# Eight conditioning dots moved from the pair stage into the middle output projection of a two-layer decoder trunk

## The chip, the cores and the metric

The kernel runs on one core of one Trainium2 chip. The metric is device microseconds of one execution. Engines are named as the profile names them: PE (TensorE matmul), PEld (its weight loads), DVE (VectorE), ACT (ScalarE), POOL (GpSimd), SP (SyncE, which only issues transfers here).

## What is computed

The reference runs two layers over x (512 tokens, 1024 channels). What matters here is the second layer:

```python
m = silu(c) @ ada_w[1] + ada_b[1]          # c: one vector of 1024
shift, scale, gate = split(m, 3)           # 1024 each
h = rmsnorm(x) * (1 + scale) + shift
gb, gc, u, g = split(h @ odd_w_in, 4)      # 2048 channels each
y = gb * (conv_b + conv3(gc * u)) * silu(g)
x = x + (1 + gate) * (y @ odd_w_out)
```

`gate` is read first where the output projection is added to x.

## The kernel before

Everything lies transposed: channels on the 128 partitions, 512 tokens along the free axis. The 2048 inner channels of layer 1 are 16 blocks j of 128. For each block four products of 128x1024 weights with h are needed. All matmuls are done in three passes on two-part numbers (hi·hi, hi·lo, lo·hi), so every weight tile is first split: ACT casts the high part, DVE subtracts to get the low part (`hilo`, L60 and L61).

**The stages of layer 1.** Blocks 0 and 1 are computed tile by tile (`classic`). From block 2 on, two weight tiles at a time form a pair and go through seven smaller products of 12 matmuls each in place of eight (`load_pair`, `prep`, `product`, `step`). A block has two pairs, the even one (gate gc and u, which ends in the convolution, `done_a`) and the odd one (gb and g, which ends in `done_b`: SiLU on ACT, two multiplications and a split on DVE). So a block is 2 x 7 x 12 = 168 matmuls of 256 columns. The order of the products is the list `order`. After the odd pair of block 8 (called the seam here; it is pair 13 of 0 to 26) the first half of the output projection stands in the list: eight tiles `("out", 0)` to `("out", 7)`, each of 24 matmuls of 512 columns, each followed by `x_add` (L225), which adds the result, scaled by the gate column of that tile, to x. Then pairs 14 to 26 follow, and the second half of the projection.

**A pair's transfers.** SP issues r2 (L879, 512 KB), r1 (L880, 512 KB) and r3 (L881, 256 KB); POOL issues one more of 512 KB that adds into r2 (L882, called the accumulating transfer here). r1 shares three buffers with the tiles of the output projection (`raw`, L74 and L75), r2 has two buffers and r3 has two. The split of a product's weights is prepared up to six steps ahead of its matmuls, into six buffers.

**The dots.** One dot of the conditioning is one row block of 128 of `silu(c) @ ada_w`: a transfer of 512 KB into one of three `araw` buffers (L107, SP), a multiply-and-sum over 128x1024 on DVE (L114) with a small read of its sum, and for the gate an addition of 1 (L124). 40 of the 48 dots are done before layer 1's pair stage. The last eight, the gate's, are done one after each of blocks 0 to 7: `ada_next(1)` in `classic` (L1015) and in `done_b` (L1031) issues the load and the dot together.

**What sets the order.** PE and SP run in the order in which the program is written. ACT, DVE and POOL are ordered by the framework's planner from its own estimates of when things are ready, and then each engine works its list in that order. `ada_dot(..., True)` pins the dot behind the DVE instruction written just before it; after a block that is the split of the block's result (`yl`, L61).

Of the kernel before, what the change touches and what calls it, by code (L numbers as in the profile page):

```python
# [37 lines left out]
class Trunk:  # L38
# [939 lines left out]
    def layer1(self):  # L978
        nc = self.nc
        ha, hb = slice(0, 256), slice(256, S)  # L980
        ra = self.ra
        hf = [self.ap.tile([P, 2, S], F32, tag="sf"[i % 2], name="hf", bufs=2) for i in range(4)]
        self.hf = [hf[k // 2][:, k % 2] for k in range(KT)]

        ws = [self.next_unit(0) for _ in range(4)]
        pj = [self.mbank() for _ in range(2)] + [self.zbank() for _ in range(2)]
        for half, sl in enumerate((ha, hb)):
            for k in range(KT):
                t = self.h_scale(1, k, ra, sl)
                self.h_hi(1, k, t, sl)  # L990
                self.h_lo(1, k, t, sl)
                nc.scalar.activation(self.hf[k][:, sl], t, AF.Identity, bias=self.adacol(1, 0, k))
                c = slice(k * P, (k + 1) * P)
                for (wh, wl), ps in zip(ws, pj):
                    self.mm3(ps[:, sl], wh[:, c], wl[:, c], self.hh[k][:, sl], self.hl[k][:, sl], k == 0, k == KT - 1)
                if half == 0 and k == 2:
                    rb = self.second()
                if half == 1 and k < 4 and k % 2:
                    self.split_upto(self.used + k // 2 + 1, True)
            ra = rb  # L1000
        ys = {}

        def classic(j, get, acc=None, sums=None):
            if acc is None:
                pc = get()
                gc = self.t512("t")
                nc.scalar.copy(out=gc, in_=pc)
                acc = self.conv(j, gc, get())
            if sums:
                sums()  # L1010
            pg = get()
            sg = self.t512("sga")
            nc.scalar.activation(sg, pg, AF.Silu)
            ys[j] = self.gated(acc, get(), sg)
            self.ada_next(1)  # L1015
            return sg

        classic(0, lambda: pj.pop(0))
        accs = {}
        self.prod_no = 0  # L1020

        def done_a(j):
            def f(gc, u):
                accs[j] = self.conv(j, gc, u)
            return f

        def done_b(j):
            def f(gb, gate):
                nc.scalar.activation(gate, gate, AF.Silu)
                ys[j] = self.gated(accs.pop(j), gb, gate)  # L1030
                self.ada_next(1)  # L1031
            return f

        pairs = []
        for j in self.PAIRED:
            pairs.append(dict(m=(16 + j, 32 + j), tag="t", done=done_a(j), odd=0, j=j))
            if j < 15:
                pairs.append(dict(m=(j, 48 + j), tag="sga", done=done_b(j), odd=1, j=j))

        order = []  # L1040
        for i, pr in enumerate(pairs):
            last = pairs[i - 1] if i else None
            order += [(pr, 1), (pr, 5)]
            if last and not last.get("early"):
                order += [(last, 4)]
            order += [(pr, 6), (pr, 2)]
            if last and not last.get("early"):
                order += [(last, 3)]
            order += [(pr, 7)]
            if pr["j"] == 8 and pr["odd"]:  # L1050
                pr["early"] = True
                order += [("out", 0), (pr, 4), (pr, 3)] + [("out", mt) for mt in range(1, 8)]
        order += [("tail", 0), (pairs[-1], 4), (pairs[-1], 3)]
        loaded = [0]

        def load_to(n):
            while loaded[0] < min(n, len(pairs)):
                pr = pairs[loaded[0]]
                pr.update(self.load_pair(*pr["m"]))
                loaded[0] += 1  # L1060

        classic(1, self.mtile, sums=lambda: (self.make_t(), load_to(1)))
        load_to(2)
        prepped = 0

        hold = [1 + next(i for i, pr in enumerate(pairs) if pr["j"] == 8 and pr["odd"])]
        for i, (pr, n) in enumerate(order):

            while prepped < min(len(order), i + 6):
                q, m = order[prepped]  # L1070
                if not isinstance(q, str):
                    if m == 1:
                        load_to(min(pairs.index(q) + 2, hold[0]))
                    if "r1" not in q:
                        break
                    self.prep(q, self.WEIGHT[m])
                prepped += 1
            if pr == "out":
                if n == 0:
                    self.limit += 8  # L1080
                if n == 6:
                    hold[0] = len(pairs)
                    load_to(loaded[0] + 1)
                w = self.next_unit(1)
                ps = self.mbank()
                self.out_mm(ps, w, [ys[q] for q in range(8)], range(8))
                self.x_add(1, n, ps)
            elif pr == "tail":
                self.limit = len(self.units)
            else:  # L1090
                self.step(pr, n)
        sg = classic(15, self.mtile, accs.pop(15))
        ys = [ys[q] for q in range(8, 16)]
        self.preload_rsqrt(sg[:, 0:1])
        ra, second = self.outproj_norm(1, ys, keep=True)

        fg = lambda k: self.cst[:, C_FG + k : C_FG + k + 1]

        def scale(k, sl):
            x = self.x[k][:, sl]  # L1100
            nc.scalar.activation(x, x, AF.Copy, scale=fg(k))

        for half, sl in enumerate((ha, hb)):
            gps = (2, 3, 4, 5) if half == 0 else (3, 4)
            tags = (("khe", "kho", "kle", "klo"), ("qe", "qo", "s", "f"))[half]
            o = [self.ap.tile([P, 2, 256], F32, tag=t, name="o", bufs=2 if t in "sf" else 1) for t in tags]
            for k in gps:
                scale(k, sl)
            if half:
                ra = second()  # L1110
            for k in (0, 3, 1, 2, 4, 5, 6, 7):
                d, x = o[k // 2][:, k % 2], self.x[k][:, sl]
                if k in gps:
                    nc.gpsimd.tensor_tensor(out=d, in0=x, in1=ra[0], op=ALU.mult)
                else:
                    nc.vector.scalar_tensor_tensor(d, x, fg(k), ra[1], ALU.mult, ALU.mult)
            for q in range(4):
                (nc.scalar if half and q == 2 else nc.sync).dma_start(self.io["out"][half, q], o[q])
# [60 lines left out]
```

## Time and profile before

| what | us |
|---|---|
| median of 3 runs (887.85 to 890.38) | 889.59 |
| the profiled execution's own time | 890.67 |
| its span, first to last instruction | 888.9 |
| mean granted TensorE clock, share of full | 0.992 |

Times in the trace count from the start of the span. In it `classic` for blocks 0 and 1 fills about 440 to 488, the pairs before the seam 488 to 649, the middle output projection 644 to 690, the pairs behind it 690 to 812. An engine's busy time counts what its instructions cover; matmuls overlap, so 100% of PE is no sign that it runs at its best rate. A wait is the idle time of an engine before an instruction, with the name of what ended it.

### The profile page before, as it was taken

How to read it: one execution, taken by the hardware profiler on the slowest of the kernel's cores; microseconds unless marked ns; L12 is line 12 of the kernel's file. 1: busy time of each engine (PE TensorE's matmuls, PEld its weight loads, DVE VectorE, ACT ScalarE, POOL GpSimd, SP SyncE). 2: the span in 40 equal slices, each digit the busy share in tenths (PEclk: the TensorE clock that was granted, in tenths of full speed). 3: DMA queues.
4: the chain of work that ended last, by engine and by line, in shares of the span. 5: the costliest groups of instructions: out<-in, count | busy, mean ns of one | idle time of the engine just before them, and what ended most of it. 6: DMA issues, size and time to landing. Idle time of an engine off the chain costs nothing.

```text
span 888.9 us, 13496 instructions
## 1 busy us (share of the span) xinstructions
PE 860.7 (97%) x5149; PEld 765.5 (86%) x5150; DVE 685.5 (77%) x1091; ACT 450.7 (51%) x821; POOL 88.0 (10%) x133
## 2 busy tenths in 40 slices
PE   8999999999999999999999899889999999999995
PEld 5788788888888888888998899889988999999885
DVE  7989978788877787695669788778854688888444
ACT  5366564655312654564465455455531556656332
POOL 2002301202000112010001101011001111110001
PEclk9999999999999999999999999999999999999998
DMA  8952132223887221223507466667555577774302
GB/s 319 300 183 67 50 107 82 60 72 119 307 276 244 75 92 51 69 72 95 166 24 190 138 194 191 177 164 193 141 159 140 151 183 175 202 180 124 116 24 94
DMA packets 41970, 128.09 MB, mean 144 GB/s; under 512 B 4273, under 2 KB 4401, under 8 KB 41906
## 3 DMA queue, kind: packets, MB, share of 16 engines
q1 hardware_dynamic: 34418, 112.82, 37.6%
q0 software_dynamic: 7344, 14.16, 9.9%
q8 instruction: 40, 0.66, 0.3%
q10 hardware_dynamic: 144, 0.26, 0.1%
q14 instruction: 24, 0.20, 0.1%
HBM read 125.13 MB, written 2.10 MB: 143 GB/s over the span
## 4 chain that ended last, share of the span: by engine, by line
PE 72%; DVE 13%; DMA 9%; ACT 3%; issue 3%; SPq 0%; DVEq 0%; ACTq 0%; POOLq 0%
PE m L190 13%; PE m L191 13%; PE m L192 13%; DMA r<-in_w1m 5%; PE zb L913 5%; PE zb L915 5%; PE zb L914 5%; DMA araw<-in_ada 3%; PE zb L669 2%; DVE wp L61 2%; PE av L400 2%; PE m L671 2%; PE z L387 1%; DVE f L371 1%; DVE araw L114 1%
## 5 line engine op out<-in xcount | busy, mean ns | idle before, releaser
L60 ACT CAST whi<-raw 128x1024 fp32r<-128x1024 f32 (+1 forms) x83 | 85.5, 1032 | 178.2 <-PE m L191 138.2
L60 ACT CAST wp<-r 128x512 fp32r<-128x512 f32 x189 | 112.7, 621 | 92.6 <-DMA r<-in_w1m 42.7
L61 DVE TENSOR_TENSOR wp<-r,wp 128x512 fp32r<-128x512 f32 x189 | 124.9, 684 | 40.3 <-ACT wp L60 39.6
L61 DVE TENSOR_TENSOR wlo<-raw,whi 128x1024 fp32r<-128x1024 f32 (+1 forms) x83 | 99.1, 1196 | 44.5 <-ACT whi L60 41.2
L913 PE MATMUL zb<-t,wp 128*128 128x256 f32 x432 | 124.5, 288 | 9.1 <-ACT sgp L932 7.1
L190 PE MATMUL m<-hh,whi 128*128 128x512 f32 x336 | 132.4, 394 | 0.6 <-DVE yt L411 0.6
L192 PE MATMUL m<-hh,wlo 128*128 128x512 f32 x336 | 131.1, 390 | 0.0
L191 PE MATMUL m<-hl,whi 128*128 128x512 f32 x336 | 131.0, 390 | 0.0
L915 PE MATMUL zb<-t,wp 128*128 128x256 f32 x432 | 123.0, 285 | 0.7 <-DVE wp L61 0.7
L914 PE MATMUL zb<-t,wp 128*128 128x256 f32 x432 | 122.9, 284 | 0.0
L190 PE MATMUL m<-yh,whi 128*128 128x512 f32 (+1 forms) x288 | 105.7, 367 | 0.0
L191 PE MATMUL m<-yl,whi 128*128 128x512 f32 (+1 forms) x288 | 105.3, 366 | 0.0
L192 PE MATMUL m<-yh,wlo 128*128 128x512 f32 (+1 forms) x288 | 105.2, 365 | 0.0
L913 PEld LDWEIGHTS zb<-t,wp 128*128 128x128 f32 x432 | 83.6, 193 | 11.7 <-ACT sgp L932 8.6
L915 PEld LDWEIGHTS zb<-t,wp 128*128 128x128 f32 x432 | 83.5, 193 | 0.9 <-DVE wp L61 0.9
L914 PEld LDWEIGHTS zb<-t,wp 128*128 128x128 f32 x432 | 83.6, 194 | 0.0
L192 PEld LDWEIGHTS m<-hh,wlo 128*128 128x128 f32 x336 | 63.1, 188 | 13.5
L190 PEld LDWEIGHTS m<-hh,whi 128*128 128x128 f32 x336 | 63.1, 188 | 13.2 <-DVE yt L411 0.8
L191 PEld LDWEIGHTS m<-hl,whi 128*128 128x128 f32 x336 | 63.2, 188 | 12.3
L225 DVE SCALAR_TENSOR_TENSOR x<-m,small,x 128x512 f32<-128x512 f32 (+1 forms) x36 | 24.8, 690 | 62.1 <-PE m L192 62.1
L365 POOL TENSOR_SCALAR_AFFINE_SELECT s<-s 128x128 f32<-128x128 f32 x64 | 43.2, 699 | 270.1 <-ACT s L360 252.3
L915 PE MATMUL zb<-hh,wp 128*128 128x256 f32 x216 | 61.8, 286 | 2.4 <-DVE wp L61 1.3
(227 smaller groups left out, 1839.1 us busy)
## 6 DMA issues: line engine op xcount, KB each, us to landing
r<-in_w1m SPq DMA_DIRECT2D x54, 512.0 KB, 4.7
raw<-in_w0m SPq DMA_DIRECT2D x36, 512.0 KB, 3.5
araw<-in_ada SPq DMA_DIRECT2D x32, 512.0 KB, 5.3
r<-in_w1m POOLq DMA_DIRECT2D x27, 512.0 KB, 6.8
ring<-in_ada SPq DMA_DIRECT2D x16, 512.0 KB, 6.0
raw<-in_w0o SPq DMA_DIRECT2D x16, 512.0 KB, 4.3
raw<-in_w1o SPq DMA_DIRECT2D x16, 512.0 KB, 3.9
r<-in_w1m SPq DMA_DIRECT2D x27, 256.0 KB, 3.3
```

The lines of the kernel that those rows point to most:

```text
L60: a = self.nc.scalar.copy(out=hi, in_=src)
L61: b = (eng or self.nc.vector).tensor_tensor(out=lo, in0=src, in1=hi.bitcast(F32), op=ALU.subtract)
L190: mm(ps, wh, xh, start=first, stop=False)
L191: mm(ps, wh, xl, start=False, stop=False)
L192: mm(ps, wl, xh, start=False, stop=last)
L225: self.nc.vector.scalar_tensor_tensor(x, ps[:, sl], self.adacol(layer, 2, mt), x, ALU.mult, ALU.add)
L365: nc.gpsimd.affine_select(out=sw[:, d], in_=sw[:, d], pattern=[[-1, P]], compare_op=ALU.is_gt, fill=0.0, base=0, channel_multiplier=1,)
L400: self.nc.tensor.matmul(ps[:, kb * P :], vs[:, kb, c : c + P], t[:, o : o + w], start=(n == 0 and kb == 0), stop=(n == 1 and kb == 3),)
L669: mm(pv[bank], h[:, tok[bank]], w[:, :512], start=f and n == 0, stop=l and n == 2)
L913: mm(ps, hi, bh, start=first and k == 0, stop=False, skip_group_check=True)
L914: mm(ps, hi, bl, start=False, stop=False, skip_group_check=True)
L915: mm(ps, lo, bh, start=False, stop=k == 3, skip_group_check=True)
```

## The change

The two calls of `ada_next(1)` are taken out. At the first step of the seam three gate loads are issued, and each of the eight output tiles does one dot, on a load of three tiles before, and issues the next load. Eight loads and eight dots stay eight loads and eight dots. In tile n the dot is written behind the split of tile n+1's weights and ahead of the tile's matmuls; `True` pins it behind that split. The load for dot n+3 reuses the buffer of dot n, so on SP it waits until dot n is done.

```diff
             ys[j] = self.gated(acc, get(), sg)
-            self.ada_next(1)
             return sg
...
                 ys[j] = self.gated(accs.pop(j), gb, gate)
-                self.ada_next(1)
             return f
...
+        seam = next(pr for pr in pairs if pr["j"] == 8 and pr["odd"])
+        gates = []
+
+        def gate_load():
+            if self.ada_rest:
+                a = self.ada_rest.pop(0)
+                gates.append((*a, self.ada_load(*a)))
+
...
-        hold = [1 + next(i for i, pr in enumerate(pairs) if pr["j"] == 8 and pr["odd"])]
+        hold = [1 + pairs.index(seam)]
...
+            if pr is seam and n == 1:
+                for _ in range(3):
+                    gate_load()
             if pr == "out":
                 if n == 0:
                     self.limit += 8
...
                 w = self.next_unit(1)
+
+                self.ada_dot(*gates.pop(0), True)
+                gate_load()
                 ps = self.mbank()
```

## Rows read from the trace of the kernel before

**Rows 1.** Page, part 1: busy us, share of the span, instructions.

```profile
PE 860.7 (97%) x5149; PEld 765.5 (86%) x5150; DVE 685.5 (77%) x1091; ACT 450.7 (51%) x821; POOL 88.0 (10%) x133
```

**Rows 2.** Windows: length, busy (instructions) by engine, PEclk, DMA share, GB/s.

```profile
505.00:508.00 3.00, 0.38 (x1) 0.38 (x2) 0.67 (x1) 1.32 (x3) 0.03 (x1) 0.82 0.73 292
508.00:511.00 3.00, 3.00 (x16) 3.00 (x16) 2.93 (x7) 1.23 (x3) 1.19 (x1) 0.50 0.33 45
...
540.00:632.00 92.00, 84.23 (x679) 81.80 (x677) 74.25 (x133) 48.10 (x102) 10.18 (x12) 1.00 0.70 190
640.00:690.00 50.00, 50.00 (x250) 42.59 (x249) 26.21 (x36) 13.68 (x18) 2.55 (x3) 1.00 0.55 148
...
715.00:796.00 81.00, 81.00 (x678) 81.00 (x676) 68.76 (x120) 48.73 (x101) 10.18 (x12) 1.00 0.71 183
```

**Rows 3.** Waits of PE, 430 to 720: total us, times, longest us.

```profile
PE zb L913 <- ACT sgp L932: 7.1, 6, 2.8
PE zb L915 <- DVE wp L61: 1.9, 2, 1.3
...
PE zb L915 <- DVE small L124: 1.1, 1, 1.1
```

**Rows 4.** Chain of work that ended last, 541 to 633: shares by line.

```profile
by line: DMA r<-in_w1m 37.2%; DMA araw<-in_ada 25.6%; DVE wp L61 11.2%; issue 7.6%; DVE araw L114 5.6%; ACT sga L1029 2.7%; ACT wp L60 2.5%; DVE u L959 1.5%; DVE t L937 1.5%; ACT sgp L932 1.1%; DVE t L949 0.8%; DVE sga L937 0.7%; DVE small 
```

**Rows 5.** The same chain, 715 to 800.

```profile
by line: PE zb L913 28.8%; PE zb L914 28.8%; PE zb L915 28.7%; PE m L914 4.7%; PE m L915 4.7%; PE m L913 4.5%
```

**Rows 6.** Tile araw, 500 to 640: dots, idle time before them, transfers.

```profile
L114 DVE CUSTOM_DVE_ANT_0 araw<-araw,cbc,cst x6: 1277/1284/1286, 526.0 to 638.3; 128x1024 f32<-128x1024 f32 x6
...
  DMA araw<-in_ada: 7.8, 5
...
DMA to landing us min/median/max: 4.9/5.7/6.8
```

**Rows 7.** Timeline of DVE around the dot of one block: start, us.

```profile
616.92 1.28 DVE L114 CUSTOM_DVE_ANT_0 araw<-araw,cbc,cst 128x1024 f32<-128x1024 f32 x1 [0.92 <-DMA araw<-in_ada]
...
618.13 0.69 DVE L61 TENSOR_TENSOR wp<-r,wp 128x512 fp32r<-128x512 f32 x1
```

**Rows 8.** Timeline of SP, pairs before the seam to the middle projection.

```profile
597.48 0.33 SPq L879 DMA_DIRECT2D r<-in_w1m  x1
...
619.51 0.33 SPq L879 DMA_DIRECT2D r<-in_w1m  x1
...
622.63 0.43 SPq L107 DMA_DIRECT2D araw<-in_ada  x1
627.84 32.69 SPq L75 DMA_DIRECT2D raw<-in_w1o  x8
660.58 0.43 SPq L879 DMA_DIRECT2D r<-in_w1m  x1
```

**Rows 9.** Timeline of DVE, blocks 0 and 1.

```profile
472.39 1.28 DVE L114 CUSTOM_DVE_ANT_0 araw<-araw,cbc,cst 128x1024 f32<-128x1024 f32 x1
...
488.71 0.68 DVE L972 TENSOR_TENSOR t<-t,m 128x512 f32<-128x512 f32 x1
...
492.32 1.28 DVE L114 CUSTOM_DVE_ANT_0 araw<-araw,cbc,cst 128x1024 f32<-128x1024 f32 x1
```

**Rows 10.** Accumulating transfer (L882) issued at 611.0, beside an araw: landing.

```profile
DMA to landing us min/median/max: 8.5/8.5/8.5
```

**Rows 11.** The same line, the 11 transfers of 690 to 815.

```profile
DMA to landing us min/median/max: 6.5/6.8/7.5
```

**Rows 12.** Waits of ACT, 715 to 796.

```profile
ACT wp L60 <- DMA r<-in_w1m: 13.6, 8, 2.0
```

**Rows 13.** Timeline of DVE in the middle output projection.

```profile
663.53 0.75 DVE L225 SCALAR_TENSOR_TENSOR x<-m,small,x 128x512 f32<-128x512 f32 x1 [3.35 <-PE m L192]
664.39 1.23 DVE L61 TENSOR_TENSOR wlo<-raw,whi 128x1024 fp32r<-128x1024 f32 x1
...
690.73 0.75 DVE L225 SCALAR_TENSOR_TENSOR x<-m,small,x 128x512 f32<-128x512 f32 x1 [2.89 <-PE m L192]
```

## The prediction

> **What bounds the kernel now.** The page's busy shares come first: PE is busy for 97% of the span [rows 1], so only what makes PE wait, or run slowly, can be won. The share is an average, so the next view is windows by stage. The pairs before and behind the seam do the same work. PE starts 679 matmuls in the 92 us from 540 to 632, and 678 in the 81 us from 715 to 796 [rows 2]. Behind the seam a matmul costs 81 / 678 = 0.1195 us and PE has no gap; ahead of it the same number takes 10.9 us more. The two stretches move about the same number of bytes per us (190 and 183 GB/s) and differ in DVE by six busy us. One thing stands ahead of the seam alone: a dot per block.
>
> The waits of PE say who ends the gaps: ACT's copy of a product's bank 7.1 us in six waits, the longest 2.8, and DVE's weight splits and the dots' small addition 3.0 us in three [rows 3]. Neither is slow; each is late. The chain of waits tells behind what. From 541 to 633 it hardly touches PE: 37.2% is the pairs' transfers, 25.6% the araw transfers, 5.6% the dots, 11.2% weight splits [rows 4]. From 715 to 800 it is PE alone [rows 5]. So the stage is a loop of transfers and DVE, and the dots lie in it: the dot is issued with its load, DVE stands still until the load lands (7.8 us in five of six cases, load to landing 5.7 us at the median), and then works on it for 1.28 us [rows 6]. One block shows it whole: 0.92 us idle, the dot from 616.92, the next weight split at 618.13 [rows 7]. Behind that split stand the release of an r2 buffer, at once SP's next r2 (619.51) [rows 8], its accumulating transfer, ACT's cast and PE.
>
> **The change part by part.**
>
> *Dots out of the pair stage.* Two counts give the worth. The first is the difference of the two stretches, 10.9 us [rows 2]. The second asks whether the loop without dots is short enough. From one r2 to that of the next block is 619.51 - 597.48 = 22.03 us [rows 8]; less 0.92 idle and 618.13 - 616.92 = 1.21 of dot [rows 7] that is 19.9. PE needs 168 x 0.1195 = 20.1 for a block. The loop falls below PE, but only just, so a gap here and there may stay; the faster landing of the accumulating transfer without an araw beside it (8.5 against 6.8 us) [rows 10, 11] helps it further. I take 10.0 of 10.9. Bound below: if only the waits that name DVE go and the transfers hold the rest, 1.3 + 1.1 = 2.4 us [rows 3]. Bound above: 10.9.
>
> *The dots of blocks 0 and 1.* They stand at 472.39 and 492.32 [rows 9], where DVE is packed. About 0.6 us of the first is of no use, since the multiplication at 488.71 also needs PE's last tile, so I count 1.21 + 0.6 = 1.8 us of earlier DVE work. Behind it stands the longest PE wait, 2.8 us [rows 3], in which PE covers only 0.38 of the 3 us from 505 [rows 2], and a short wait of 0.6 for a weight split (1.9 less 1.3) [rows 3]. The short one goes, 0.6; PE then reaches the long one 0.6 sooner and it ends 1.8 sooner, so 1.2 goes there: 1.8 in all. In the 2.8 us gap the granted clock falls to the lower level, 0.50 or 1.2 GHz, and PE starts 16 matmuls in 3 us [rows 2], where it starts 3 / 0.1195 = 25, or some 27 counted with those that reach in. Over the two such windows I estimate 2 x 12 x 0.12 = 2.9 us. A gap of 1.6 us is left; the waits of up to 1.3 us later in the stage [rows 3] left the clock at 1.00 in the whole of 540 to 632 [rows 2]. 1.6 is nearer to 1.3 than to 2.8, but PE coming sooner may only meet the loop sooner, so I take half, 1.5. Bounds: 0, and 2.8 + 0.6 + 2.9 = 6.3.
>
> *Three loads at the seam.* On SP they follow the seam pair's own loads, where one araw stands now (622.63) [rows 8], so two are added just ahead of the seam's accumulating transfer. One araw beside such a transfer made it 8.5 us and not 6.8, +1.7 [rows 10, 11]. Two more would make it 1.7 to 3.4 later. What hides it: behind the seam ACT waits for this transfer up to 2.0 us with PE unbroken [rows 12, 2], and the loop without dots gives some tenths a block. I take a loss of 1.5, bounds 0 and 3 x 1.7 = 5.1. The Trainium skill (DMA: Bandwidth & Descriptors, section Queues, rings and completion order) says that each transfer engine takes turns between the queues that have work, packet by packet; the trace agrees as far as the +1.7 goes. By that rule a 512 KB transfer on POOL's queue is held by about its own amount from SP's, however much waits there, and the loss would be at most 1.7 and the sum 0.2 lower at worst than mine; by the linear count it would be 3.6 lower.
>
> *Eight dots in the middle projection.* DVE waits 3.35 us for PE before `x_add`, tile after tile, a tile being (690.73 - 663.53) / 5 = 5.44 us [rows 13]; a dot takes 1.28 us [rows 6], with its small operations at most 1.5 (my estimate), and fits. The split of tile 5's weights at 664.39 ends 8 us before that tile starts (663.53 + 2 x 5.44 = 674.4), so a dot ahead of a split moves nothing either. Without that cover the dots would cost at most 8 x 1.5 = 12 us. PE is covered for all of 640 to 690 [rows 2].
>
> *Five loads more on SP, and what queues behind them.* The load for dot 7 waits for dot 4. Behind it on SP stand the transfers of pairs 14 and 15, which now start at 660.58 [rows 8]. Dot 4 is pinned behind the split of tile 5, at 664.39 [rows 13], so it ends near 667.1 and pair 14 starts some 7 us later, at 667.5. With 4 us for r2 (my estimate below the 5.7 of an araw in company) and 8.5 for the accumulating transfer [rows 10] it is there at 680; PE asks for it after 690.73 [rows 13]. DMA's share of 0.55 over 640 to 690 [rows 2] leaves room: 8 x 512 KB in 50 us add 84 GB/s to 148. Cost 0, bounds 0 and 2.
>
> **Sum.** 10.0 + 1.8 + 1.5 - 1.5 = 11.8 us. The profiled execution took 890.67, so it would take 878.9; the median of the runs shown is 1.1 lower, which gives 877.8.
>
> **Rivals.**
>
> *The gaps stay (13 in 100).* The pairs' transfers hold the loop by themselves. For it: they are the chain's largest share [rows 4], and 19.9 is close to 20.1. Against: the same transfers behind the seam leave PE without a gap [rows 5]. It gives 2.4 + 1.8 - 1.5 = 2.7 us, 886.9.
>
> *The seam pays (13 in 100).* The three loads make the accumulating transfer 5.1 us late and PE stops there, as at 505 long enough to fall to the lower clock level (1.5 more): 10.0 + 1.8 + 1.5 - 5.1 - 1.5 = 6.7, 882.9. For it: PE waits for that transfer already at 632. Against: the cover of 2.0 us.
>
> *SP is held in the projection: slower (4 in 100).* The planner could place dot 4 far later than right behind its pin. Each us later than 667 + 10 = 677 makes pair 14, and with it PE, one us late. To eat the 11.8 it must stand at 689 or later, and for over 0.3%, about what a measurement of this kernel can tell from no change, at 692. Against: `x_add` of tile 4 needs that dot and stands near 674.4 [rows 13].
>
> *It changes nothing (4 in 100).* The planner, with other instructions to place, could order ACT's casts so that a copy again stands behind a late transfer in every block. Gains of the first part then go to new waits of the same size: 888 to 891.
>
> **How the numbers follow.** The forecast holds 66 in 100, with gains of 8.5 to 17 us (10.9 + 6.3 at best), 872.5 to 881. Taking in the second rival, the range goes to 884 and holds 8 in 10. Faster: 66 + 13 + 10 of the first rival's 13 = 0.89, same 0.03 + 0.04 = 0.07, slower 0.04.
>
> **What would show it.** Right: 679 matmuls ahead of the seam in about 82 us, the chain there on PE, no PE wait over 0.5 us from 520 to the seam, r2 to r2 of the next block near 20.2 us, a PE wait of at most 2 us at the seam, PE full in the projection, dots without idle time before them. Wrong: waits of PE on ACT's copies that repeat every block, an accumulating transfer of over 10 us at the seam with a longer PE wait behind it, or r2 of pair 14 issued later than 677 from now's clock.

## The result, and the profile after

The changed kernel takes 879.04 us at the median (876.13 to 881.49, 4 runs), the kernel before on the same chip 888.72 (886.67 to 890.38): a ratio of 0.9891, 95% interval 0.9845 to 0.9937. That is 9.7 us less; 11.8 were forecast. Its times spread more widely than the changes to be told apart below, and the profiled execution is the longest of the four, 881.49 us with a span of 879.5. The page's parts 1 and, of part 4, the first line:

```profile
PE 857.2 (97%) x5149; PEld 764.0 (87%) x5150; DVE 685.8 (78%) x1091; ACT 452.9 (52%) x821; POOL 88.0 (10%) x133
...
PE 74%; DVE 11%; DMA 10%; ACT 3%; issue 3%; SPq 0%; DVEq 0%; ACTq 0%
```

PE's share is the same 97% as in [rows 1], of a span that is 9.4 us shorter. Windows of the changed kernel (columns as in [rows 2]):

```profile
531.00:612.00 81.00, 80.69 (x671) 80.49 (x671) 68.92 (x122) 48.67 (x101) 10.18 (x12) 1.00 0.71 185
618.00:621.00 3.00, 0.20 (x2) 0.00 (x0) 0.21 (x1) 0.86 (x2) 0.00 (x0) 1.00 0.50 184
621.00:624.00 3.00, 2.40 (x15) 2.40 (x16) 2.97 (x6) 2.51 (x7) 0.00 (x0) 0.78 0.00 0
624.00:627.00 3.00, 3.00 (x19) 3.00 (x19) 2.97 (x7) 1.55 (x5) 0.00 (x0) 0.65 0.00 0
631.00:681.00 50.00, 50.00 (x249) 42.52 (x248) 33.22 (x52) 13.34 (x17) 2.55 (x3) 1.00 0.61 191
```

In 81 us ahead of the seam PE now starts 671 matmuls, nearly the 678 of the stretch behind it; before it needed 92 us for 679 [rows 2]. The projection holds the eight dots (DVE busy 33.2 us in its 50, before 26.2) and PE has no gap in it. Between the two, from 618, PE stands still and then runs partly at the lower clock. PE's waits of 430 to 720 (columns as in [rows 3]):

```profile
PE zb L913 <- ACT sgp L932: 4.8, 2, 3.4
PE zb L913 <- ACT u L941: 0.6, 2, 0.3
...
```

Six waits on the copy have become two, one of 1.4 us near 505 and one of 3.4 at the seam. The timeline of SP at the seam (start, us, instruction):

```profile
608.92 1.39 SPq L107 DMA_DIRECT2D araw<-in_ada  x3
```

and of ACT, with its idle time before an instruction and what ended it:

```profile
620.14 0.62 ACT L60 CAST wp<-r 128x512 fp32r<-128x512 f32 x1 [5.84 <-DMA r<-in_w1m]
...
621.20 0.35 ACT L932 COPY sgp<-zb 128x256 f32<-128x256 f32 x1
```

The copy that PE waits for (L932) needs nothing that is late. It stands in ACT's queue behind a cast that waits 5.84 us for the seam's accumulating transfer. The kernel before had the same stop at the seam, smaller: its cast waited 3.50 us and PE 1.06, at 632.47.

```profile
631.01 0.62 ACT L60 CAST wp<-r 128x512 fp32r<-128x512 f32 x1 [3.50 <-DMA r<-in_w1m]
```

In the changed kernel the chain of waits, 600 to 645, has the seam's transfer in it (start, us, what):

```profile
608.96 11.12 DMA r<-in_w1m
```

The order of PE's matmuls is the same in both kernels, so the same matmul can be found in both traces and its start times subtracted. That gives the lead of the changed kernel along the way, and a ledger of the change (start times from the two traces):

```
matmul   before    after    lead
 2419    491.85   491.43    0.42
 2525    507.62   505.79    1.84   block 1's wait shorter
 2551    513.33   509.00    4.33   no lower clock there
 2778    541.26   536.87    4.39
 3113    586.60   577.68    8.92   gaps of the pair stage gone
 3401    625.39   612.28   13.11
 3449    632.47   621.60   10.87   stop at the seam
 3473    635.44   626.02    9.42   lower clock behind it
 5148    879.99   870.52    9.47   the last one
```

### The profile page after: what moved, and what is told of

Its sections match the earlier page's. It is cut to its first block, busy times and chain, and to the rows that moved or that the text cites. A ratio compares the mean times of both kernels' runs of the same rounds, so it can differ in the third digit from the quotient of the medians.

```text
span 879.5 us, 13504 instructions
## 1 busy us (share of the span) xinstructions
PE 857.2 (97%) x5149; PEld 764.0 (87%) x5150; DVE 685.8 (78%) x1091; ACT 452.9 (52%) x821; POOL 88.0 (10%) x133
## 4 chain that ended last, share of the span: by engine, by line
PE 74%; DVE 11%; DMA 10%; ACT 3%; issue 3%; SPq 0%; DVEq 0%; ACTq 0%
PE m L190 14%; PE m L191 14%; PE m L192 14%; DMA r<-in_w1m 9%; PE zb L913 5%; PE zb L915 5%; PE zb L914 5%; DVE wp L61 2%; PE zb L669 2%; PE av L400 2%; PE m L671 2%; PE z L387 2%; DVE f L371 1%; PE z L356 1%; PE zb L814 1%
## 5 line engine op out<-in xcount | busy, mean ns | idle before, releaser
L190 PEld LDWEIGHTS m<-yh,whi 128*128 128x128 f32 x288 | 54.3, 189 | 8.8
```

Source lines behind the costliest of these rows:

```text
L190: mm(ps, wh, xh, start=first, stop=False)
```

## Experiments

All times are medians. The first four ran on one chip beside each other, with the kernel before at 890.17 us; the other six on a second chip, four beside the kernel before at 890.1 and the last two at another time, beside 888.66.

| run | what | us (lowest to highest) |
|---|---|---|
| e1_after_again | changed kernel | 879.01 (876.57 to 881.04) |
| e2_late | three loads behind the seam's transfer | 875.51 (874.88 to 875.90) |
| e3_one | one load at the seam | 876.43 (874.92 to 877.94) |
| e4_none | no gate dots, no loads | 875.31 (874.77 to 876.97) |
| e5_ahead | dots in place, loads two ahead | 883.12 (881.44 to 885.82) |
| e6_transfers | loads in place, no dots | 879.40 (878.33 to 881.20) |
| e7_dots | dots in place, no loads | 880.77 (879.71 to 882.19) |
| e8_before_look5 | before, splits five steps ahead | 889.89 (886.01 to 892.29) |
| e10_late_two_back | late loads, two dots back | 878.84 (877.62 to 880.90) |
| e11_five | 2.5 MB at the seam | 879.49 (875.47 to 881.91) |

**The stop at the seam.** The theory: the three loads hold the accumulating transfer, and with it ACT and PE. The rival: the stop belongs to the seam, which had a wait before too.

> The changed kernel once more, beside the others. Both theories: 876 to 881 us. If the stop at the seam is caused by the three gate loads, it is there in this profile too: the accumulating transfer there lands after about 11 us and PE waits 2 to 3.5 us.

The time came, the size of the stop did not: the transfer landed after 8.9 us here, not 11, and PE waited 1.1 us (and no lower clock followed). So the stop varies from execution to execution, and with it the time: 876.57 here, 881.49 in the first profile. Of the 5.0 us between the two, 3.8 arise at the seam, by the start times of their matmuls. What makes the transfer take 8.9 us in one execution and 11.1 in another no run shows.

```diff
# e2_late, against the changed kernel
-            if pr is seam and n == 1:
-                for _ in range(3):
-                    gate_load()
...
                 if n == 0:
                     self.limit += 8
+                    self.load_upto(self.used + 2)
+                    for _ in range(3):
+                        gate_load()
```

> The three gate loads stand on SP behind the load of the second output tile and so start after the seam's accumulating transfer has landed. Theory (the three loads hold that transfer): it lands in under 7.5 us, PE's wait at the seam falls from 3.4 us to under 1, the lower clock there is gone, 4 to 5 us less than the changed kernel's profile, 874 to 877 us. Rival (the stop belongs to the seam, whoever loads): PE still waits 2 us or more, 879 to 881 us.

As the theory has it. The transfer at the seam lands after 6.8 us, the cast waits 1.36 us for it, and the same copy behind it (at 616.39) holds nobody up:

```profile
615.33 0.62 ACT L60 CAST wp<-r 128x512 fp32r<-128x512 f32 x1 [1.36 <-DMA r<-in_w1m]
```

Of PE's waits of 430 to 720 these are left:

```profile
PE zb L913 <- ACT sgp L932: 1.2, 1, 1.2
PE zb L913 <- ACT u L941: 0.3, 1, 0.3
```

The one of 1.2 us is block 1's, near 505. At the seam there is none (windows of 612 to 621, each 3.00 us of PE in 3.00; one is shown), and the chain from 526 to 607 is PE's, as it was behind the seam in [rows 5]:

```profile
615.00:618.00 3.00, 3.00 (x27) 3.00 (x27) 2.31 (x5) 2.44 (x5) 0.00 (x0) 1.00 0.52 175
```

```profile
by line: PE zb L913 29.3%; PE zb L915 28.3%; PE zb L914 28.3%; PE m L913 4.7%; PE m L914 4.7%; PE m L915 4.7%; issue 0.0%
```

All six runs lie below all six of the changed kernel on the same chip. The ratio to the kernel before is 0.9844 (0.9813 to 0.9875), the lowest of the kernels that compute all of it.

```diff
# e3_one, against the changed kernel
-                for _ in range(3):
+                for _ in range(1):
                     gate_load()
```

> One gate load at the seam in place of three, each next one a tile ahead. Theory: the transfer at the seam lands after 8 to 8.5 us, PE waits about 1 us there, and dots in the projection wait up to 1 us for their loads, hidden: 875 to 878 us. Rival (the wait grows with no relation to the number of loads): wait of 3 us and 879 to 881.

The time is as the theory has it. The transfer takes 8.9 us and PE waits 1.5 us at the seam, both more than expected and no less than in e1 with three loads; no dot waits for its load. That fewer loads cost less thus rests on the times, 874.92 to 877.94 here and 876.57 to 881.04 with three, and not on this one profile.

```diff
# e4_none, against the changed kernel
+        nc.vector.memset(self.ada[:, 40:48], 1.0)
         classic(0, lambda: pj.pop(0))
...
-            if pr is seam and n == 1:
-                for _ in range(3):
-                    gate_load()
...
-                self.ada_dot(*gates.pop(0), True)
-                gate_load()
```

> Leaves out the eight gate dots and their loads altogether (the gate columns are set to 1), so it shows what they cost in their new place. Theory: no stop at the seam, all else as in the changed kernel, 874 to 877 us, and no more than 1 us under the kernel with late loads. Rival (the projection pays for the dots): 2 us or more under the kernel with late loads.

0.2 us under e2_late: with late loads, the eight dots in the projection cost nothing that can be measured. The changed kernel pays 3.7 us for them at the median, nearly all of it (3.5) gone when the three loads come late. The stop at the seam is not wholly gone without loads: the transfer took 7.8 us in this profile and PE waited 0.4 us.

```diff
# e11_five, against the changed kernel
                 for _ in range(3):
                     gate_load()
+                for q, tag in enumerate(("qe", "qo", "khe", "kho")):
+                    spare = self.ap.tile([P, S], F32, tag=tag, name="spare")
+                    nc.sync.dma_start(spare, self.io["ada"][1, 16 + q, :, :512])
```

> The changed kernel with 1 MB more of loads at the seam, behind the three gate loads, into buffers that are idle there and are never read: 2.5 MB in place of 1.5 in SP's queue ahead of and beside the accumulating transfer. If that transfer is held in proportion to all that waits in SP's queue (1.7 us for 0.5 MB): landing after 13 to 16 us, PE's wait 6 us or more, 882 to 885 us. If queues take turns and hold it by no more than its own amount: landing stays at 9 to 11.5 us, the time at 877 to 881.

The landing of the seam's transfer in e11_five (line L882, 606.5 to 608):

```profile
DMA to landing us min/median/max: 11.1/11.1/11.1
```

2.5 MB in SP's queue hold it no longer than 1.5 MB did at worst, 11.1 us both, and the median, 879.49, is near that of the changed kernel, 879.01; the count in proportion, 882 or more, is refuted. The times, 875.47 to 881.91, scatter a little more widely than those of the changed kernel.

One profile of each kernel gives, for the seam (us):

| profile | landing of the transfer | wait of ACT's cast for it | stop of PE |
|---|---|---|---|
| before | 6.7 | 3.50 | 1.06 |
| changed | 11.1 | 5.84 | 3.40 |
| e1_after_again | 8.9 | 3.50 | 1.07 |
| e2_late | 6.8 | 1.36 | none |
| e3_one | 8.9 | 3.93 | 1.50 |
| e4_none | 7.8 | 2.81 | 0.38 |
| e11_five | 11.1 | 5.30 | 2.87 |

In all six with a stop, the stop is the cast's wait less 2.4 us: so much of the wait is covered, and each further us of it is a us of PE. With the transfer at 6.8 us 1.36 of these 2.4 are already used up, and 1.1 are left.

The queues show how the transfer comes to 11.1 us. Packets, MB and share of the 16 engines of SP's queue (q1) and POOL's (q0), in the first profile of the changed kernel from 609 to 614 and from 614 to 620, and of POOL's in e2_late from 611 to 615:

```profile
q1 hardware_dynamic: 411, 1.25, 82.1%
q0 software_dynamic: 13, 0.03, 3.0%
```

```profile
q1 hardware_dynamic: 305, 1.10, 48.9%
q0 software_dynamic: 259, 0.50, 47.1%
```

```profile
q0 software_dynamic: 257, 0.49, 76.2%
```

In e2_late the transfer, issued at 608.5, moves its 0.49 MB in the 4 us from 611. In the changed kernel, issued at 609.0, it moves almost nothing before 614, while SP's loads move 1.25 MB, and then its 0.50 MB in 6 us, at an even share with SP's queue. So it is late in two ways, by a later start and by sharing; why it starts later is open.

**What the dots cost where they were.** The three parts of a dot, each by itself in the kernel before:

```diff
# e5_ahead: `fetch(), fetch()` ahead of block 0 (fetch issues a load), then in place of self.ada_next(1):
+            if ahead:
+                self.ada_dot(*ahead.pop(0), True)
+                fetch()
...
# e6_transfers, in place of self.ada_next(1):
+            if self.ada_rest:
+                self.ada_load(*self.ada_rest.pop(0))
...
# e7_dots, in place of self.ada_next(1):
...
+                ins = nc.vector.tensor_tensor_reduce(
+                    out, self.cbc, self.cbc, 1.0, self.cst[:, b : b + 1], ALU.mult, ALU.add, col
+                )
+                self.tc.keep_in_program_order(ins)
+                nc.vector.tensor_scalar_add(col, col, 1.0)
```

> The kernel before, its eight dots where they were, but each load issued two blocks ahead, so that no dot waits for its load. Theory (the wait of the dot and DVE's time lie in the loop in about equal parts): DVE's idle time before dots 0, about half of the 10 us of gaps gone, 882 to 886 us. Rival (the transfers' bytes are what holds the loop): under 1.5 us gained, 887 to 889.

> The kernel before with the eight loads where they were and no dots at all (leaves out the gate dots; the gate columns are set to 1). Theory: the loads alone cost little, PE's gaps of 520 to 632 shrink to under 2 us, 876 to 879 us. Rival (bytes): gaps stay, 884 us or more.

> The kernel before with the eight dots where they were, on data that lies in the memory of the core, and no loads for them (the gate values are thus not those of the reference). Theory: DVE's 1.21 us per block remain in the loop, its waits are gone: PE's gaps 2 to 5 us in all, 879 to 884 us. Rival (only the wait for the load matters): as without dots, 875 to 877 us.

e5 and e7 came as the theory has them in time; e6 lies 0.4 us above its range and far from the rival. PE's waits are more than expected in both: in the loop from 520 to 632 3.1 us in e6 (under 2 expected), and from 440 to 720 5.7 us in e7 (2 to 5 expected), of which 2.3 lie in the loop and 3.4 at blocks 0 and 1 (one of 2.7 us, with the lower clock behind it). With e4_none (875.31, the chips' kernels before 0.1 us apart) as the floor, and the loop and blocks 0 and 1 taken together, loads alone cost 4.1 us, dots alone 5.5, both without the wait 7.8, and both with the dot waiting for its load, as before, 14.8. So 7.0 of the 14.8 go when no dot waits for its load; the rest is work and transfers in a loop that has little to spare, and they overlap in part. In e5_ahead the waits before dots are gone and PE still waits on the copies, nearly as long as before (7.1 us [rows 3]):

```profile
PE zb L913 <- ACT sgp L932: 7.0, 6, 2.1
...
```

so issuing the loads earlier, alone, would have won less than half.

**ACT's order as the rival cause.** In [rows 3] most gaps end with ACT's copy. If ACT's order were the cause, writing the cast one step later would cure it.

```diff
# e8_before_look5, against the kernel before
-            while prepped < min(len(order), i + 6):
+            while prepped < min(len(order), i + 5):
```

> The kernel before, weights of a product prepared five steps ahead instead of six, so that ACT's copy of a bank is written ahead of the cast that waits for the accumulating transfer. Theory (the dots are in the loop; ACT's order only passes the wait on): gaps shrink by at most 4 us, 885 to 889 us. Rival (ACT's order is the cause): the PE waits on that copy go and the time falls by 7 us or more, 878 to 882.

Ratio 0.9997 (0.9979 to 1.0015): no change. But the edit did not do what it was meant to. The planner left ACT's list as it was: in the trace one copy of 815 casts, copies and activations changes its place (L926, near 497), and the copy that PE waits for still stands behind the cast that waits for the transfer, as at 631.01 and 632.07 in the kernel before:

```profile
630.44 0.62 ACT L60 CAST wp<-r 128x512 fp32r<-128x512 f32 x1 [2.95 <-DMA r<-in_w1m]
...
631.50 0.35 ACT L932 COPY sgp<-zb 128x256 f32<-128x256 f32 x1
```

So this run does not test the rival. e2_late bears on it: there ACT's list has the order of the kernel before from 500 on, and PE has no wait from 520 to 720. The order alone thus makes no gap; it takes a late transfer with it. Whether another order would have hidden the lateness with the dots in place was not tried.

**The dots of blocks 0 and 1.**

```diff
# e10_late_two_back, against e2_late
             ys[j] = self.gated(acc, get(), sg)
+            if j < 2:
+                self.ada_next(1)
...
-                self.ada_dot(*gates.pop(0), True)
+                if gates:
+                    self.ada_dot(*gates.pop(0), True)
                 gate_load()
```

> The kernel with late loads, but the dots of blocks 0 and 1 back behind those blocks, six moved. By the prediction's term these two are worth 3.3 us (1.8 of waits and half of the lower clock), by the matmuls' start times in the changed kernel 4.3: 878.8 to 879.8 us, with PE's wait near 507 back at 2 us or more and a stretch at the lower clock behind it. Rival (the loop gives the time back later, since PE only meets it sooner): 876 to 877 us.

878.84 against 875.51, 3.3 us, though on two chips: by the ratios to the kernel before, 0.9868 and 0.9844, it is 2.1 us, and their intervals (0.9833 to 0.9904 and 0.9813 to 0.9875) overlap, so the size is not shown. The profile has both parts of the term, a PE wait of 3.3 us up to 508 and the lower clock behind it:

```profile
PE zb L913 <- ACT sgp L932: 3.3, 1, 3.3
...
```

```profile
508.00:511.00 3.00, 2.68 (x12) 2.68 (x13) 2.93 (x6) 1.93 (x4) 1.22 (x1) 0.50 0.30 47
```

By the start times of the same matmuls, this run lies 0.5 us behind e2_late at 466.7, 5.1 at 519.97 and 4.3 at 621.85. So 0.8 us of what is lost at blocks 0 and 1 comes back in the pairs, as the rival has it, and the rest does not.

## Why the prediction was right, and which term was mis-sized

The direction, the mechanism and the range held. The sum was 10.0 + 1.8 + 1.5 - 1.5 = 11.8; by the ledger of the two profiles it is 9.8 + 1.8 + 2.5 - 4.8 = 9.3. That the sum came so near is in part luck. The gains were taken too low, 13.3 for 14.1 in the ledger (14.7 by the medians of before and e2_late), and the loss at the seam too low as well, 1.5 for 4.8 (3.5 by the medians of e1 and e2_late); the two errors partly cancel. The ledger is also that of the slowest execution of the four: beside e1 the same two kernels are 890.17 - 879.01 = 11.2 us apart.

- **Dots out of the pair stage**, taken at 10.0: the lead grows from 4.39 to 13.11, 8.7 us, and the wait of 1.1 us at matmul 3449 of before, which the comparison of the two stretches had partly in it, makes it 9.8. (DVE's busy time differs by 5.5 us between those stretches, not by six.) The step from r2 to r2 of the next block fell from 22.03 us [rows 8] to 20.2 (574.86 to 595.08), the bound that PE sets. That the loop without dots lies only just under PE showed twice: small waits of 0.3 us stay, and putting loads or dots back alone brings waits of 3.1 and 2.3 us back into it (e6, e7).
- **Dots of blocks 0 and 1**, 1.8 and 1.5: the waits gave 1.84. The clock term was halved for doubt; the wait shrank to 1.39 us, the clock stayed at its upper level, and the whole 2.5 came. Of these 4.3 us the run with the two dots put back found 2 to 3.3 in the time of the kernel.
- **Three loads at the seam**, 1.5, is the mis-sized step. In the profile the stop is 3.40 us and the stretch at 1.2 GHz behind it costs 13.11 - 9.42 less the 2.2 of the stop itself, 1.5 more; with the wait of before that is no longer there, 4.8. The bounds (0 to 5.1) held it, and the second rival, taken at 13 in 100, had the mechanism to the letter: the transfer late, PE stopped, the clock down. Two things were wrong. The two further loads made the transfer up to 4.3 us later than 6.8, where 1.7 to 3.4 were expected (2.1 in e1, and 2.1 with a single load). And the cover of 2.0 us was read behind the seam: at the seam it is 2.4, but the kernel before had used it up already (a wait of 3.50, a stop of 1.06), and with the loop without dots only 1.1 were left (e2_late). So PE stopped for 1.1 us in e1 and for 3.4 in the first profile. Here the prediction's own sign of being wrong, a transfer of over 10 us at the seam with a longer wait of PE behind it, came in the first profile and not in e1. The loss is some 1 us or 5 us by execution, and with late loads the spread of the changed kernel's times goes too (e2_late: six runs within 1.0 us).
- **The rule of the page** (the Trainium skill, DMA: Bandwidth & Descriptors, section Queues, rings and completion order): the page says that an engine takes turns between the queues that have work. The trace agrees where both queues move data, from 614 to 620 (48.9 and 47.1%), and so do the 11.1 us with 1.5 MB and with 2.5. But turns are not all of the 4.3 us, since POOL's queue moved almost nothing in the five us before. Nor do they stand behind the +1.7 on which the prediction leaned: beside the araw of [rows 10], SP's queue moved 0.66 MB from 612 to 615 and POOL's nothing, and from 615 to 619 POOL's moved its 0.52 MB beside 0.13. That transfer started late and was hardly shared with. So 1.7 was no measure of the bound.
- **Eight dots in the projection**, 0: no dot waited for its load, PE has no gap, and e4_none puts the cost at 0.2. The cover was thinner than the 3.35 us of the prediction: `x_add` waits 1.9 us or more for PE in five tiles, 0.3 in the first two and not at all in the last.
- **SP held in the projection**, 0: pair 14's r2 went from 660.58 [rows 8] to 657.86, with a lead of 9.4 thus 6.7 us later, as worked out (7), and PE saw none of it.
- The rival that the gaps stay is refuted by the windows. The sign that the chain ahead of the seam would lie on PE failed for the changed kernel (from 531 to 612 it is 69.1% the pairs' transfers), because the late transfer at the seam pulls the chain back into the transfers; without it (e2_late) it holds.

## What to carry to other kernels

In this kernel a load issued together with its use cost the wait, the work and the bytes, since the loop lies just at the bound of the busiest engine; moving the work to a stage where its engine idles removed them, and by the medians prefetching alone about half. A prefetch has to be placed by what is in flight where it starts: three loads in front of a transfer with little slack gave back a quarter of the gain, and the same three loads 15 us later gave back nothing that could be measured. To find such a loss, subtract the start times of the same instruction in two traces; the place where the lead shrinks is the place to look. And when an experiment changes an order in the program, read from its trace whether the engine's order changed: in e8 it had not.

## What the runs showed of the hardware that was not expected

An accumulating transfer of 512 KB on POOL's queue, beside the pair's own loads, took 6.8 and 7.8 us with no gate load on SP's queue (e2_late, e4_none), 8.9 with 0.5 MB of them (e3_one), 8.9 and 11.1 in two executions with 1.5 MB, and 11.1 with 2.5. A late start was part of it: in the first profile of the changed kernel POOL's queue moved 0.03 MB in the five us after the issue, and then the rest at an even share with SP's. Stops of PE of up to 1.6 us in the pair stage left the granted clock at its upper level in every profile here. After those of 2.7 to 3.4 us (five profiles) PE ran for a stretch at 1.2 GHz. Between, a stop of 2.1 us did so too (e5_ahead), and stops of 2.1 and 2.3 us did not (e8_before_look5). A stop has no fixed price either: the 2.8 us of before cost 2.5 more behind it, the 3.4 us of after 1.5 more.
